# A depthwise convolution whose running sums stand in two PSUM banks, inside a two-layer transformer trunk

## The chip, the cores and the metric

The kernel runs on one core of a Trainium2 chip. The core has a matrix engine (TensorE, "PE" in the profile, with its weight loads as "PEld"), three elementwise engines (VectorE "DVE", ScalarE "ACT", GpSimd "POOL"), a queue engine that starts transfers (SyncE, "SP"), an on-chip memory SBUF and the accumulators PSUM: eight banks, each 128 partitions of 512 fp32 words. Each engine executes its own instructions in program order and waits on semaphores where an operand or a buffer comes from another engine. The metric is the device time of one execution in microseconds (us).

## What is computed

Two layers over 256 tokens of width 1024. Each layer normalises its input and multiplies it by one combined projection matrix. Half of the columns feed an attention of eight heads with three branches (compressed blocks, selected blocks, a sliding window); the other half, 2 × 512 columns, feed a gated causal convolution. Both results go through one output projection, and a channel mixer follows: a dense one in layer 0, one of eight experts in layer 1. The change touches the convolution:

```python
CONV_KERNEL = 31
def conformer_conv(u, conv_w, conv_b, ln_g, ln_b):
    a, g = jnp.split(u, 2, axis=-1)
    h = a * jax.nn.sigmoid(g)
    h = jnp.pad(h, ((0, 0), (CONV_KERNEL - 1, 0), (0, 0)))
    y = lax.conv_general_dilated(h, conv_w[:, None, :], window_strides=(1,), padding='VALID',
                                 dimension_numbers=('NWC', 'WIO', 'NWC'),
                                 feature_group_count=CONV_WIDTH)
    y = y + conv_b
    return jax.nn.silu(layer_norm(y, ln_g, ln_b))
```

Each of the 512 channels is thus a sum of 31 shifted copies of its own row, each times its own weight, and the attention shares with it only the input and the output projection. Of the attention's compressed branch the beginning matters here: the compressed keys and values `kv` are cut into 15 overlapping blocks of 32 tokens and multiplied by a hidden matrix (`compress_blocks`).

## The kernel before, in words

Channels lie on partitions: the 512 channels of the convolution are four chunks `c` of 128 partitions by 256 tokens, in two pairs. TensorE computes the 2 × 256 columns of a pair in 16 steps (`conv_proj`, a step `uA` for pair 0, `uB` for pair 1) into a tile `pu` of two PSUM banks; each step has two chunks of three matmuls (high and low parts, lines 275 to 277). When a pair is complete, `glu` (line 581) writes the gated rows to `hpad` in SBUF.

The 31 taps are divided between two engines. `tap_v` (lines 590 and 593) does the first 17 taps of pair 0 and 16 of pair 1 on VectorE: one instruction multiplies a shifted row of 128 × 256 by a weight per partition and adds the running sum `cv`, in SBUF. `tap_g` does the other taps: ScalarE multiplies (line 602) and GpSimd adds to another sum `cvg` (line 603). `ln_merge` (`lm0`, `lm1`, line 925) adds the two sums of a pair, and a layer norm over channels follows.

Beside this stands the compressed branch. Its projection `pkv` has two banks: the first holds keys and values, ScalarE copies it to `kvc`, and TensorE multiplies this by a permutation (`swap`, line 737) into the second. VectorE copies pieces of both to `blk` (`blk_part`, line 744); 16 × 4 small matmuls `ph` (line 774) follow, and VectorE's `hx` (line 782) reads these. The scores of a step are `S0` to `S11` (tile `pss`, with VectorE's minimum `nm`, line 704), the probabilities `P0` to `P11` (transposes `ptp`, line 844), the values `V0` to `V11` (tile `po`).

The order of all engines in an attention stage is written by hand as a list of tokens, `SEQ`, which is run through once per layer; nothing reorders it. `v` and `g` are one tap each on VectorE and on ScalarE with GpSimd. The PSUM pools have two buffers each: `pa` and `pb` of one bank, `pacc` of two banks (four banks in all). From `pacc` come, in this order, `pkv`, `pu` of pair 0, `pu` of pair 1, the values `po` of the two token blocks and the output projection `pout`. A buffer is given to a new tile when all readers and writers of its last tile are done, and the first instruction that writes the new tile waits for that.

```python
    pacc = ctx.enter_context(tc.tile_pool(name="pacc", bufs=2, space=PSUM))
    def acc_bank(name="acc"):
        return pacc.tile([P, 2, 512], F32, name=name, tag="acc")
    def mm3(dst, ah, al, bh, bl, start, stop, skip=False):
        nc.tensor.matmul(dst, ah, bh, start=start, stop=False, skip_group_check=skip)
        nc.tensor.matmul(dst, ah, bl, start=False, stop=False, skip_group_check=skip)
        nc.tensor.matmul(dst, al, bh, start=False, stop=stop, skip_group_check=skip)
```

In the built program `pkv` stands in banks 4 and 5, `pu` of pair 0 in 6 and 7, and `pu` of pair 1 in 6 and 7 again.

Of the kernel before, what the change touches and what calls it, by code (L numbers as in the profile page):

```python
# [11 lines left out]
F32 = mybir.dt.float32  # L12
# [36 lines left out]
NPT = (0, 0)  # L49
# [6 lines left out]
    P4 S6 P5 v v v g V3 S7 v cs1 g g v cp0 g g S8 g v V4 P6 g g P7 g g join0 S9 cv0 cp1 v V5 v g g V6 v turn0 g g  # L56
    v v v lm0 g V7 oa g P8 g g P9 S10 S11 g V8 v v oa P10 g P11 v v v v V9 v V10 v v lm1 V11 join1 lmean cv1 oa
# [12 lines left out]
def trunk(ctx: ExitStack, tc: tile.TileContext, x, positions, attn_norm_g, ffn_norm_g, w_in, w_out,  # L70
# [397 lines left out]
    for layer in range(DEPTH):  # L468
# [90 lines left out]
        def conv_proj(pair, n):  # L559
            part, k = divmod(n, DK)  # L560
            if n == 0:
                pus[pair] = acc_bank("pu").rearrange("p c (i t) -> p c i t", i=2)
# [42 lines left out]
        pcv = {}  # L605

        def tap_p(pair, j, first, last):

            cs_ = slice(2 * pair, 2 * pair + 2)
            if first:  # L610
                pcv[pair] = bank_a("pcv").rearrange("p (c t) -> p c t", c=2)
            dg = sm.tile([P, 2, P], F32, name="dg", tag="tap", bufs=3)
            nc.gpsimd.tensor_tensor(dg, ident[:, None, :].to_broadcast([P, 2, P]),
                                    cw5[layer][:, cs_, j:j + 1].to_broadcast([P, 2, P]), op=ALU.mult)
            for c in range(2):
                nc.tensor.matmul(pcv[pair][:, c], dg[:, c], hpad[:, 2 * pair + c, j:j + S],
                                 start=(first and c == 0), stop=last, skip_group_check=True)

        vs, gs, ps = [], [], []
# [947 lines left out]
```

## Time and profile before

| | before |
|---|---|
| median of 3 runs | 1595.72 us (1594.69 to 1595.79) |
| the profiled execution | 1595.13 us |
| its span | 1593.3 us |
| busy: TensorE, VectorE, ScalarE, GpSimd | 96%, 84%, 69%, 8% of the span |
| attention stage of layer 0, 40 to 160 us | TensorE 109.36 of 120.00 us busy, VectorE 106.11, ScalarE 75.78, GpSimd 52.73; granted clock 0.86 |
| attention stage of layer 1, 440 to 560 us | TensorE 111.41 of 120.00 us busy, VectorE 106.85, ScalarE 77.04, GpSimd 51.64; granted clock 0.82 |
| dense mixer, 160 to 440 us | TensorE 273.74 of 280.00 us busy |
| experts, 560 to 1593 us | TensorE 1012.81 of 1033.00 us busy |

Times in the trace count from the start of the span; the profiled execution is 1.8 us longer than its span. [...] Busy times overlap between engines. A matmul's recorded length overlaps the next one, so the distance between two starts says more than the length. VectorE's records overlap a little too.

### The profile page before, as it was taken

The page shows a single profiled execution, that of the slowest core. Times are in us where ns is not written, and L with a number is a line of the kernel's source. Part 1 is how long each engine was busy: PE and PEld are TensorE (multiplying, and loading weights), DVE is VectorE, ACT ScalarE, POOL GpSimd, SP SyncE. Part 2 cuts the span into 40 slices and gives each one's busy share as a digit, 9 for nine tenths or more (in the row PEclk, how much of TensorE's full clock was granted, in tenths as well). Part 3 has the DMA queues.
Part 4 walks back from the last instruction along what each step waited for, and adds up shares of the span by engine and source line. Part 5 has one row for each costly group of instructions (what it writes and reads, how often), then busy time and mean ns, then how long its engine had stood idle before and what let it go on. Part 6 is the DMA issues. An engine that isn't in the chain of part 4 may idle for free.

```text
span 1593.3 us, 21310 instructions
## 1 busy us (share of the span) xinstructions
PE 1534.5 (96%) x7833; PEld 1289.9 (81%) x7833; DVE 1337.6 (84%) x1637; ACT 1093.3 (69%) x1430; POOL 122.1 (8%) x152
## 2 busy tenths in 40 slices
PE   6989999999998989999999999999999999999997
PEld 5977799999798768887887887887887887888885
DVE  7898655455689879999999999899999999999996
ACT  5765544444466557787777887787787777778774
POOL 2443000000045300000000000000000000000000
PEclk9978999999997789999999999999999999999999
DMA  9700584555632039999999999999999999999991
GB/s 308 230 28 1 170 315 172 185 186 179 166 122 91 27 120 342 366 367 334 346 369 346 373 370 339 337 361 350 369 369 346 328 362 351 366 369 363 355 371 40
DMA packets 197744, 433.75 MB, mean 272 GB/s; under 512 B 10346, under 2 KB 28978, under 8 KB 197636
## 3 DMA queue, kind: packets, MB, share of 16 engines
q1 hardware_dynamic: 196902, 432.02, 75.8%
q8 instruction: 63, 1.03, 0.3%
q0 software_dynamic: 288, 0.30, 0.1%
q14 instruction: 45, 0.37, 0.1%
q10 hardware_dynamic: 446, 0.03, 0.0%
HBM read 431.27 MB, written 1.05 MB: 271 GB/s over the span
## 4 chain that ended last, share of the span: by engine, by line
PE 80%; DVE 14%; ACT 3%; issue 2%; DMA 1%; POOL 0%; SPq 0%; DVEq 0%; ACTq 0%
PE pg L275 12%; PE pg L277 12%; PE pg L276 12%; PE pd L277 8%; PE pd L276 8%; PE pd L275 7%; DVE cv L593 4%; DVE wl L190 4%; PE pgu L275 3%; PE pgu L277 3%; PE pgu L276 3%; PE pt L288 2%; ACT wh L189 1%; PE pgx L1246 1%; DVE nm L704 1%
## 5 line engine op out<-in xcount | busy, mean ns | idle before, releaser
L190 DVE TENSOR_TENSOR wl<-raw,wh 128x1024 fp32r<-128x1024 f32 x808 | 976.3, 1224 | 176.6 <-ACT wh L189 147.9
L189 ACT CAST wh<-raw 128x1024 fp32r<-128x1024 f32 x808 | 845.4, 1052 | 302.4 <-PE pg L277 102.6
L275 PE MATMUL pg<-wh,xgH 128*128 128x512 f32 x896 | 351.2, 392 | 0.0
L277 PE MATMUL pg<-wh,xgL 128*128 128x512 f32 x896 | 350.6, 391 | 0.0
L276 PE MATMUL pg<-wl,xgH 128*128 128x512 f32 x896 | 349.9, 391 | 0.0
L275 PE MATMUL pd<-wh,fh 128*128 128x512 f32 x560 | 225.8, 403 | 0.1
L276 PE MATMUL pd<-wl,fh 128*128 128x512 f32 x560 | 221.5, 396 | 1.3 <-DVE wl L190 1.3
L277 PE MATMUL pd<-wh,fl 128*128 128x512 f32 x560 | 221.9, 396 | 0.0
L277 PEld LDWEIGHTS pg<-wh,xgL 128*128 128x128 f32 x896 | 168.4, 188 | 35.9 <-DVE xgL L1250 0.2
L276 PEld LDWEIGHTS pg<-wl,xgH 128*128 128x128 f32 x896 | 168.6, 188 | 34.9 <-DVE wl L190 0.3
L275 PEld LDWEIGHTS pg<-wh,xgH 128*128 128x128 f32 x896 | 168.6, 188 | 34.0
L277 PEld LDWEIGHTS pd<-wh,fl 128*128 128x128 f32 x560 | 105.3, 188 | 25.0 <-DVE fl L272 0.2
L276 PEld LDWEIGHTS pd<-wl,fh 128*128 128x128 f32 x560 | 105.4, 188 | 24.6 <-DVE wl L190 2.0
L275 PEld LDWEIGHTS pd<-wh,fh 128*128 128x128 f32 x560 | 105.4, 188 | 22.7 <-ACT fh L271 0.3
L275 PE MATMUL pgu<-hFH,wh 128*128 128x256 f32 x384 | 108.9, 284 | 0.8 <-DVE posT L452 0.8
L277 PE MATMUL pgu<-hFH,wl 128*128 128x256 f32 x384 | 108.7, 283 | 0.0
L276 PE MATMUL pgu<-hFL,wh 128*128 128x256 f32 x384 | 108.7, 283 | 0.0
L603 POOL TENSOR_TENSOR cvg<-cvg,tap 128x256 f32<-128x256 f32 x108 | 93.5, 891 | 80.1 <-ACT tap L602 76.3
L593 DVE SCALAR_TENSOR_TENSOR cv<-hpad,cw,cv 128x256 f32<-128x256 f32 x124 | 75.1, 658 | 0.0
L275 PEld LDWEIGHTS pgu<-hFH,wh 128*128 128x128 f32 x384 | 73.7, 192 | 1.1 <-PE pgk L1080 0.9
L276 PEld LDWEIGHTS pgu<-hFL,wh 128*128 128x128 f32 x384 | 73.7, 192 | 0.2
L277 PEld LDWEIGHTS pgu<-hFH,wl 128*128 128x128 f32 x384 | 73.7, 192 | 0.0
(369 smaller groups left out, 1656.8 us busy)
## 6 DMA issues: line engine op xcount, KB each, us to landing
raw<-in_moe_w_gate_dram SPq DMA_DIRECT2D x112, 1024.0 KB, 5.3
raw<-in_moe_w_up_dram SPq DMA_DIRECT2D x112, 1024.0 KB, 5.4
raw<-in_moe_w_down_dram SPq DMA_DIRECT2D x112, 1024.0 KB, 4.9
raw<-in_w_in_dram SPq DMA_DIRECT2D x18, 1024.0 KB, 9.5
raw<-in_ffn_w_gate_dram SPq DMA_DIRECT2D x14, 1024.0 KB, 7.5
raw<-in_ffn_w_up_dram SPq DMA_DIRECT2D x14, 1024.0 KB, 4.9
raw<-in_ffn_w_down_dram SPq DMA_DIRECT2D x14, 1024.0 KB, 4.9
raw<-in_w_out_dram SPq DMA_DIRECT2D x8, 1024.0 KB, 10.6
```

What stands on the lines that cost most here:

```text
L189: nc.scalar.copy(h, r)
L190: nc.vector.tensor_tensor(lo, r, h.bitcast(F32), op=ALU.subtract)
L275: nc.tensor.matmul(dst, ah, bh, start=start, stop=False, skip_group_check=skip)
L276: nc.tensor.matmul(dst, ah, bl, start=False, stop=False, skip_group_check=skip)
L277: nc.tensor.matmul(dst, al, bh, start=False, stop=stop, skip_group_check=skip)
L288: nc.tensor.transpose(pt[:, k], src[:, k * P:(k + 1) * P], ident)
L593: nc.vector.scalar_tensor_tensor(cv[:, c], src, cw5[layer][:, c, j:j + 1], cv[:, c], op0=ALU.mult, op1=ALU.add)
L603: nc.gpsimd.tensor_tensor(cvg[:, c], cvg[:, c], tap, op=ALU.add)
L704: nc.vector.tensor_reduce(nm, pss, AX.X, ALU.min)
L1246: nc.tensor.matmul(pgx, src[:, b, k * P:(k + 1) * P], ohs[pair][:, b].rearrange("p e s -> p (e s)"), start=(m == 0 and b == 0), stop=(m == ...
```

## The change

The running sums of VectorE, `cv`, are written to a tile `pcv` of two PSUM banks that holds all four chunks. The first call of `tap_v` takes from the pool `pacc` first the tile `pu` of pair 1 and then `pcv`; `conv_proj` then finds the `pu` of pair 1 already there. A new token `leave` ends the use of `pcv`: sums that come after it are written to `cv` in SBUF, and the first one of each chunk reads `pcv`. `lm0` reads pair 0 from `pcv`. In `SEQ`, `leave` and `lm0` with four `v` stand ahead of the token `S8`; `V4` to `V6` and `turn0` have lost the `v` between them, and `lm0` no longer follows `turn0`. A third way of doing taps on TensorE (`tap_p`), whose count `NPT` was zero, is taken out.

```diff
-    P4 S6 P5 v v v g V3 S7 v cs1 g g v cp0 g g S8 g v V4 P6 g g P7 g g join0 S9 cv0 cp1 v V5 v g g V6 v turn0 g g
-    v v v lm0 g V7 oa g P8 ...
+    P4 S6 P5 v v v g V3 S7 v cs1 g g v leave lm0 cp0 v v v v g g S8 g V4 P6 g g P7 g g join0 S9 cv0 cp1 V5 g g V6 turn0 g g
+    v v v g V7 oa g P8 ...
...
-            if n == 0:
+            if n == 0 and pair not in pus:
                 pus[pair] = acc_bank("pu").rearrange("p c (i t) -> p c i t", i=2)
...
+        pcv, sums = {}, {}
+
         def tap_v(c, j):
             src = hpad[:, c, j:j + S]
+            if not pcv:
+                pus[1] = acc_bank("pu").rearrange("p c (i t) -> p c i t", i=2)
+                pcv["t"] = acc_bank("pcv").rearrange("p a (c t) -> p (a c) t", c=2)
+            dst = cv[:, c] if pcv["t"] is None else pcv["t"][:, c]
             if j == 0:
-                nc.vector.tensor_scalar(cv[:, c], src, cw5[layer][:, c, 0:1], cw[layer][:, c, 31:32],
+                nc.vector.tensor_scalar(dst, src, cw5[layer][:, c, 0:1], cw[layer][:, c, 31:32],
                                         op0=ALU.mult, op1=ALU.add)
             else:
-                nc.vector.scalar_tensor_tensor(cv[:, c], src, cw5[layer][:, c, j:j + 1], cv[:, c],
+                nc.vector.scalar_tensor_tensor(dst, src, cw5[layer][:, c, j:j + 1], sums[c],
                                                op0=ALU.mult, op1=ALU.add)
+            sums[c] = dst
+
+        def conv_leave():
+
+            pcv["both"], pcv["t"] = pcv["t"], None
...
         def ln_merge(pair):
             c = slice(2 * pair, 2 * pair + 2)
-            if NPT[pair]:
-                nc.vector.tensor_tensor(cv[:, c], cv[:, c], pcv[pair], op=ALU.add)
-            if NDT[pair] + NPT[pair] < CONV_K:
-                nc.vector.tensor_tensor(cv[:, c], cv[:, c], cvg[:, c], op=ALU.add)
+            assert not vs[pair] and not gs[pair]
+            src = cv[:, c] if pair else pcv["both"][:, c]
+            nc.vector.tensor_tensor(cv[:, c], src, cvg[:, c], op=ALU.add)
```

In the changed program `pkv` stands in banks 4 and 5, `pu` of pair 0 in 6 and 7, `pcv` in 6 and 7 and `pu` of pair 1 in 4 and 5.

TensorE around the start of `pu` of pair 1, with the semaphores each instruction waits for. `pg` is the projection of the gates, `swapm` the permutation of `kvc`. Before:

```order
L275 MATMUL pg<-hTH,wgH_612 24x256
L276 MATMUL pg<-hTL,wgH_612 24x256
L277 MATMUL pg<-hTH,wgL_613 24x256
L737 MATMUL pkv<-kvc,swapm 128x512 [waits Activation_49]
L275 MATMUL pu<-hTH,wh 128x256 [waits DVE_49]
L276 MATMUL pu<-hTL,wh 128x256
L277 MATMUL pu<-hTH,wl 128x256
```

In the changed program:

```order
L274 MATMUL pg<-hTH,wgH_612 24x256
L275 MATMUL pg<-hTL,wgH_612 24x256
L276 MATMUL pg<-hTH,wgL_613 24x256
L731 MATMUL pkv<-kvc,swapm 128x512 [waits Activation_49]
L274 MATMUL pu<-hTH,wh 128x256 [waits DVE_49,PE_49]
L275 MATMUL pu<-hTL,wh 128x256
L276 MATMUL pu<-hTH,wl 128x256
```

The order of the matmuls is the same. The first one into `pu` waited for VectorE's `glu` of pair 0, the last reader of that bank pair; it now waits for the last reader of `pkv`, VectorE's last copy into `blk`.

VectorE from `glu` of pair 0 to that copy. `cw_604` holds the taps' weights, `cw_603` the bias, `posT_616` the position term. Before:

```order
L581 SCALAR_TENSOR_TENSOR hpad<-th,pu 128x256 [waits Activation_49] x2
L590 TENSOR_SCALAR cv<-hpad,cw_604,cw_603 128x256 [waits DVE_49] x2
L593 SCALAR_TENSOR_TENSOR cv<-hpad,cw_604,cv 128x256 [waits DVE_49] x7
L744 COPY blk<-kvc 64x16x15 [waits Activation_49]
L744 COPY blk<-pkv 64x16x15 [waits PE_49]
L744 COPY blk<-pkv 64x16x15
L744 COPY blk<-kvc 64x16x15
L747 COPY blk<-posT_616 128x16
L593 SCALAR_TENSOR_TENSOR cv<-hpad,cw_604,cv 128x256 [waits DVE_49]
L744 COPY blk<-kvc 64x16x15
L744 COPY blk<-pkv 64x16x15 x2
```

In the changed program:

```order
L580 SCALAR_TENSOR_TENSOR hpad<-th,pu 128x256 [waits Activation_49] x2
L596 TENSOR_SCALAR pcv<-hpad,cw_604,cw_603 128x256 [waits DVE_49] x2
L599 SCALAR_TENSOR_TENSOR pcv<-hpad,cw_604,pcv 128x256 [waits DVE_49] x7
L738 COPY blk<-kvc 64x16x15 [waits Activation_49]
L738 COPY blk<-pkv 64x16x15 [waits PE_49]
L738 COPY blk<-pkv 64x16x15
L738 COPY blk<-kvc 64x16x15
L741 COPY blk<-posT_616 128x16
L599 SCALAR_TENSOR_TENSOR pcv<-hpad,cw_604,pcv 128x256 [waits DVE_49]
L738 COPY blk<-kvc 64x16x15
L738 COPY blk<-pkv 64x16x15 x2
```

Nothing moved here; the sums have another tile, and the wait of each on VectorE itself is for the sum right in front of it, where it was for the one two places ahead.

VectorE where `leave` and `lm0` stand, around the probabilities of the compressed branch (`pcmp`, `rsum`, `cfc`) and the minimum of S8. Before:

```order
L884 TENSOR_REDUCE rsum<-pcmp 128x8 [waits Activation_49]
L886 TENSOR_SCALAR cfc<-rsum 128x8 [waits DVE_49]
L887 RECIPROCAL cfc<-cfc 128x8 [waits DVE_49]
L888 TENSOR_TENSOR cfc<-cfc,gate 128x8 [waits DVE_49]
L704 TENSOR_REDUCE nm<-pss 128x2 [waits PE_49]
L593 SCALAR_TENSOR_TENSOR cv<-hpad,cw_604,cv 128x256
```

In the changed program:

```order
L599 SCALAR_TENSOR_TENSOR pcv<-hpad,cw_604,pcv 128x256
L918 TENSOR_TENSOR cv<-pcv,cvg 128x512 [waits DVE_49]
L878 TENSOR_REDUCE rsum<-pcmp 128x8 [waits Activation_49]
L880 TENSOR_SCALAR cfc<-rsum 128x8 [waits DVE_49]
L881 RECIPROCAL cfc<-cfc 128x8 [waits DVE_49]
L882 TENSOR_TENSOR cfc<-cfc,gate 128x8 [waits DVE_49]
L599 SCALAR_TENSOR_TENSOR cv<-hpad,cw_604,pcv 128x256 x2
L599 SCALAR_TENSOR_TENSOR cv<-hpad,cw_604,cv 128x256 [waits DVE_49] x2
L698 TENSOR_REDUCE nm<-pss 128x2 [waits PE_49]
```

The merge and four sums moved ahead of the minimum of S8. On TensorE the first matmul of V4 (`po<-v_sb,prT`), which waited for nothing of VectorE before, now waits for VectorE's second sum after `leave`, the last reader of `pcv`, since `po` of the second token block takes its banks. The other engines' order is the same.

## Rows read from the trace of the kernel before

**Rows 1.** The page's part on the chain that ended last: shares of the span by engine, then by engine, tile and line.

```profile
PE 80%; DVE 14%; ACT 3%; issue 2%; DMA 1%; POOL 0%; SPq 0%; DVEq 0%; ACTq 0%
PE pg L275 12%; PE pg L277 12%; PE pg L276 12%; PE pd L277 8%; PE pd L276 8%; PE pd L275 7%; DVE cv L593 4%; DVE wl L190 4%; PE pgu L275 3%; PE pgu L277 3%; PE pgu L276 3%; PE pt L288 2%; ACT wh L189 1%; PE pgx L1246 1%; DVE nm L704 1%
```

**Rows 2.** Busy time of each engine in the stretch with the second projection and the first half of the taps, in layer 0 and in layer 1: stretch, its length, then busy us (x instructions) of PE, PEld, DVE, ACT, POOL, the granted clock, the share of the DMA engines, GB/s.

```profile
62.00:88.50 26.50, 26.16 (x184) 25.10 (x182) 26.39 (x40) 16.15 (x34) 18.64 (x20) 0.83 0.37 125
463.30:491.40 28.10, 27.70 (x185) 26.91 (x184) 27.95 (x45) 19.02 (x43) 18.64 (x20) 0.78 0.30 102
```

**Rows 3.** The timeline of TensorE and VectorE where TensorE first stands idle, four rows of layer 0 and three of layer 1: start, duration of the group, engine, line, operation, tiles, shape, count, and in brackets the idle time ahead and what ended it.

```profile
88.84 1.42 PE L844 MATMUL ptp<-ident,sc 128*128 128x128 f32 x4 [0.32 <-DVE gate L757]
90.05 3.46 PE L774 MATMUL ph<-blk,raw 128*128 128x31 f32 x16
95.24 0.22 DVE L782 COPY hx<-ph 128x62 f32<-128x62 f32 x1
95.47 1.11 PE L844 MATMUL ptp<-ident,sc 128*128 128x128 f32 x4 [1.96 <-ACT prT L846]
...
492.24 2.11 PE L774 MATMUL ph<-blk,raw 128*128 128x31 f32 x16
496.88 0.21 DVE L782 COPY hx<-ph 128x62 f32<-128x62 f32 x1
497.11 1.12 PE L844 MATMUL ptp<-ident,sc 128*128 128x128 f32 x4 [2.77 <-ACT prT L846]
```

**Rows 4.** The timeline of TensorE at the start of `pu` of pair 1, with the same columns; the last row is that of layer 1.

```profile
61.97 0.68 PE L275 MATMUL pu<-hTH,wh 128*128 128x256 f32 x1
62.49 0.28 PE L276 MATMUL pu<-hTL,wh 128*128 128x256 f32 x1
...
463.28 0.68 PE L275 MATMUL pu<-hTH,wh 128*128 128x256 f32 x1
```

**Rows 5.** The timeline of VectorE from the first sum to the last copy out of `pkv`, with the same columns; the last row is that copy in layer 1.

```profile
61.26 0.73 DVE L590 TENSOR_SCALAR cv<-hpad,cw,cw 128x256 f32<-128x256 f32 x2
61.90 4.30 DVE L593 SCALAR_TENSOR_TENSOR cv<-hpad,cw,cv 128x256 f32<-128x256 f32 x7
...
69.12 1.03 DVE L593 SCALAR_TENSOR_TENSOR cv<-hpad,cw,cv 128x256 f32<-128x256 f32 x1
70.08 0.36 DVE L744 COPY blk<-kvc 64x240 f32<-64x240 f32 x1
70.45 0.82 DVE L744 COPY blk<-pkv 64x240 f32<-64x240 f32 x2
...
471.77 0.82 DVE L744 COPY blk<-pkv 64x240 f32<-64x240 f32 x2
```

**Rows 6.** The timelines of GpSimd's additions and of two groups of sums on VectorE, one beside them and one where GpSimd has none; the same columns.

```profile
63.12 6.75 POOL L603 TENSOR_TENSOR cvg<-cvg,tap 128x256 f32<-128x256 f32 x8 [15.02 <-ACT tap L602]
70.63 12.02 POOL L603 TENSOR_TENSOR cvg<-cvg,tap 128x256 f32<-128x256 f32 x12 [0.76 <-ACT tap L602]
```
```profile
73.35 3.58 DVE L593 SCALAR_TENSOR_TENSOR cv<-hpad,cw,cv 128x256 f32<-128x256 f32 x4
...
84.39 2.05 DVE L593 SCALAR_TENSOR_TENSOR cv<-hpad,cw,cv 128x256 f32<-128x256 f32 x5
```

**Rows 7.** The timeline of VectorE at two operations of the compressed scores, of which the second reads what the first writes.

```profile
115.29 0.29 DVE L870 TENSOR_TENSOR scmp<-psc,scmp 128x128 f32<-128x128 f32 x1
115.61 0.29 DVE L872 TENSOR_REDUCE mncmp<-scmp 128x8 f32<-128x128 f32 x1
```

**Rows 8.** All the running sums, and the scaling of the layer norm, whose operand `prs` is in PSUM: line, engine, operation, tiles, count, duration of one in ns (minimum, median, maximum), first and last start.

```profile
L593 DVE SCALAR_TENSOR_TENSOR cv<-hpad,cw,cv x124: 463/479/1046, 61.9 to 540.3; 128x256 f32<-128x256 f32 x124
L955 DVE SCALAR_TENSOR_TENSOR cv<-cv,cw,prs x8: 473/475/482, 147.3 to 551.3; 128x256 f32<-128x256 f32 x8
```

**Rows 9.** TensorE's clock: two pairs of neighbouring matmuls of `pu` in the timeline, then the busy times and the granted clock (the third number from the end) of two stretches of layer 0 and two of layer 1.

```profile
74.35 0.28 PE L276 MATMUL pu<-hTL,wh 128*128 128x256 f32 x1
74.46 0.28 PE L277 MATMUL pu<-hTH,wl 128*128 128x256 f32 x1
...
86.39 0.41 PE L275 MATMUL pu<-hTH,wh 128*128 128x256 f32 x1
86.61 0.41 PE L276 MATMUL pu<-hTL,wh 128*128 128x256 f32 x1
```
```profile
80.00:84.00 4.00, 4.00 (x19) 3.79 (x19) 4.00 (x6) 0.51 (x1) 2.65 (x4) 0.50 0.03 6
88.80:93.50 4.70, 4.66 (x20) 4.14 (x20) 4.70 (x11) 3.89 (x18) 2.46 (x3) 0.50 0.01 3
488.70:491.40 2.70, 2.70 (x14) 2.70 (x15) 2.67 (x9) 1.85 (x10) 0.00 (x0) 0.50 1.04 400
491.40:494.50 3.10, 2.95 (x21) 2.83 (x20) 3.10 (x5) 2.62 (x12) 2.46 (x3) 0.79 0.46 175
```

**Rows 10.** The timeline of layer 0 behind `hx`: three groups of VectorE's sums, and TensorE's output projection with the idle time ahead of it.

```profile
98.04 0.92 DVE L590 TENSOR_SCALAR cv<-hpad,cw,cw 128x256 f32<-128x256 f32 x1
109.78 1.35 DVE L593 SCALAR_TENSOR_TENSOR cv<-hpad,cw,cv 128x256 f32<-128x256 f32 x2
111.65 2.31 DVE L593 SCALAR_TENSOR_TENSOR cv<-hpad,cw,cv 128x256 f32<-128x256 f32 x3
...
128.34 0.50 PE L277 MATMUL pout<-wh,mixL 128*128 128x512 f32 x1 [1.43 <-DVE mixL L272]
```

More of the change, by code (lines that the diff above doesn't have):

```diff
@@ L48 @@
 NDT = (17, 16)
-NPT = (0, 0)
 SEQ = """
@@ L55 @@
     P0 ph3 v g P1 gelu v g S2 heads v g g g v g P2 S3 S4 cnorm V0 g v v V1 v keys v g S5 v g P3 cs0 v g g v V2 g
-    P4 S6 P5 v v v g V3 S7 v cs1 g g v cp0 g g S8 g v V4 P6 g g P7 g g join0 S9 cv0 cp1 v V5 v g g V6 v turn0 g g
-    v v v lm0 g V7 oa g P8 g g P9 S10 S11 g V8 v v oa P10 g P11 v v v v V9 v V10 v v lm1 V11 join1 lmean cv1 oa
+    P4 S6 P5 v v v g V3 S7 v cs1 g g v leave lm0 cp0 v v v v g g S8 g V4 P6 g g P7 g g join0 S9 cv0 cp1 V5 g g V6 turn0 g g
+    v v v g V7 oa g P8 g g P9 S10 S11 g V8 v v oa P10 g P11 v v v v V9 v V10 v v lm1 V11 join1 lmean cv1 oa
     lvar turn1 lscale oa oa lout oa oa oa
@@ L603, in tap_g @@
                 nc.gpsimd.tensor_tensor(cvg[:, c], cvg[:, c], tap, op=ALU.add)
[L605 to L619, printed above, removed]
+        vs, gs = [], []
         for pair in range(2):
             nd = NDT[pair]
-            ng = nd + NPT[pair]
             vs.append([lambda c=c, j=j: tap_v(c, j) for j in range(nd) for c in (2 * pair, 2 * pair + 1)])
-            ps.append([lambda pair=pair, j=j, nd=nd, ng=ng: tap_p(pair, j, j == nd, j == ng - 1)
-                       for j in range(nd, ng)])
-            gs.append([lambda c=c, j=j, ng=ng: tap_g(c, j, j == ng) for j in range(ng, CONV_K)
+            gs.append([lambda c=c, j=j, nd=nd: tap_g(c, j, j == nd) for j in range(nd, CONV_K)
                        for c in (2 * pair, 2 * pair + 1)])
@@ L1000, in trunk @@
                  "oc": [lambda k=k, b=b: out_conv(k, b) for b in range(NB) for k in range(4)],
-                 "p": [lambda: some(ps, 1)] * (2 * CONV_K),
                  "v": [lambda: some(vs, 1)] * (4 * CONV_K), "g": [lambda: some(gs, 1)] * (4 * CONV_K),
@@ L1023, in trunk @@
         events += [("gelu", cmp_gelu), ("heads", cmp_heads), ("cnorm", cmp_norm), ("keys", cmp_keys)]
-        events += [("lm0", lambda: ln_merge(0)), ("lm1", lambda: ln_merge(1)), ("lmean", ln_mean), ("lvar", ln_var), ("lscale", ln_scale), ("lout", ln_out)]
+        events += [("leave", conv_leave), ("lm0", lambda: ln_merge(0)), ("lm1", lambda: ln_merge(1)), ("lmean", ln_mean), ("lvar", ln_var), ("lscale", ln_scale), ("lout", ln_out)]
         for b in range(NB):
```

## The prediction

> **What bounds the kernel now.** I read the chain of waits first [rows 1]. It gives TensorE 80% of the span and VectorE 14%, and names the running sums of the convolution (`cv`, line 593) with 4%, as if they were worth shortening. An average over stages can't say that, so I read the table of busy time for the stage in which the sums stand. From 62.00 to 88.50 TensorE is busy 26.16 of 26.50 us and VectorE 26.39; in layer 1, from 463.30 to 491.40, 27.70 and 27.95 of 28.10 [rows 2]. Both are full. Which one decides is seen in the order of time. TensorE's first idle of more than a trace is 0.32 us at 88.84; the next that counts is 1.96 us ahead of 95.47, and in layer 1 2.77 us ahead of 497.11 [rows 3]. Up to there VectorE is late, but TensorE has other work in its order and loses nothing. What VectorE saves before 88.8 therefore buys at most the little that TensorE waits for it: 0.32 us, and the time by which VectorE's `hx` is behind the matmuls `ph` that feed it, 95.24 − (90.05 + 3.46) = 1.73 us; in layer 1 496.88 − (492.24 + 2.11) = 2.53 us [rows 3]. I call these the slack: 2.05 us in layer 0, 2.5 in layer 1.
>
> **The change part by part.** *1. The buffers.* The pool of accumulators has two buffers of two banks. Before, the bank pair of `pkv` stays with the compressed keys while the second projection `pu` takes the pair that the first has left, so TensorE starts it at 61.97 (layer 1: 463.28) [rows 4]. The changed order gives that pair to `pcv`, and the second `pu` gets the pair of `pkv`. Its first matmul now waits for VectorE's last read of `pkv`. In the order this copy stands behind two sums that begin a chunk, eight that go on, and the other copies into `blk`; in the trace it ends at 70.45 + 0.82 = 71.27, in layer 1 at 471.77 + 0.82 = 472.59 [rows 5]. TensorE works in order, so everything behind that matmul (the rest of `pu`, the gates, the transposes, S0, `ph`) stands as well.
>
> How long: VectorE's own work ahead of the copy changes too. Seven sums take 4.30 us and one takes 0.96 until the copy behind it starts (69.12 to 70.08) [rows 5]. They contend with GpSimd's additions `cvg`: without these a sum comes each 0.40 us (five from 84.39 in 2.05, the last being 0.47 long), beside them each 0.88 (four from 73.35 in 3.58) [rows 6]. In the changed order each sum waits for the one right in front of it, because four chunks share one tile, where before it waited for the one two places ahead. A dependent operation follows after its full length and 0.03 us (115.29, 0.29 long, to 115.61) [rows 7], so I take 0.48 + 0.03 = 0.51 for each sum into PSUM, with no contention. Seven then take 3.57 (−0.7), the single one 0.40, as a copy from another tile follows it (−0.56), the two that begin a chunk 0.24 more than the 0.64 between 61.26 and 61.90 [rows 5]. Together −1.0: the copy ends at 70.2. The stall is 70.2 − 61.97 = 8.3, less 0.4, since the matmul that leads now costs 0.52 to the next (61.97 to 62.49) [rows 4] and only some 0.12 once it starts warm: **7.9 us** in layer 0; in layer 1 472.59 − 1.0 − 463.28 = 8.3, and also 7.9.
>
> No row shows a VectorE sum into PSUM. The nearest is line 955, which reads one operand from PSUM: 473, 475 and 482 ns at minimum, median and maximum, against a median of 479 for the sums in SBUF, which go up to 1046 [rows 8]. So the length is taken as 0.48 and the contention as gone. Bounds: no serialization (0.40 apart) makes the stall 1.0 shorter, the contended pace of 0.88 makes it 3.8 longer (nine sums by 0.37, and the start).
>
> [...]
>
> *2. What the stall is worth.* The slack takes its part: 7.9 − 2.05 = 5.85 in layer 0, 7.9 − 2.5 = 5.4 in layer 1. VectorE, which was late, uses the stall to catch up, so `hx` then follows `ph` at once.
>
> *3. TensorE's clock.* Nowhere else in the two attention stages does TensorE stand for nearly 8 us. [...] I expect the lower level after such a pause. How soon the upper returns with dense `pu` work is seen in layer 1: from 488.70 to 491.40 the granted clock is 0.50 and from 491.40 to 494.50 0.79 on average, which is 2.7 + 3.1 × 0.42 = 4.0 us at the lower level [rows 9]. Four microseconds hold 18 matmuls at 0.22, and 18 × (0.215 − 0.12) is **1.75 us** per layer. Bounds: 0, and the lower level through all 96 matmuls of the second `pu`, 9.1 us.
>
> *4. Sums behind the stall.* From 95 us on VectorE sets the pace. The start of a chunk at 98.04 takes 0.92 where it takes 0.41 alone; two sums at 109.78 take 1.35 and three at 111.65 2.31, against 0.88 and 1.28 at 0.40 apart [rows 10]: −0.5 − 0.5 − 1.0 = −2.0 if PSUM ends contention. Five dependent sums in this stretch at +0.11 give 0.55 back. **−1.4 us** per layer; layer 1 taken as the same.
>
> *5. The merge and four sums, moved.* `lm0` and four sums go from behind V5, V6 and the first transposes to ahead of S8. Their number is the same, and V4 and the minimum of S8 come later by the merge, 0.6, and four sums, 1.6, which the 1.4 and the later gap repay; cost 0. Bounds for 4 and 5 together: +0.7 per layer less gain (S8 waits and nothing comes back), and −2.8 in all if also TensorE's 1.43 us ahead of 128.34 [rows 10] goes. The first matmul of V4 now waits for VectorE's second sum, which is over long before: 0. The first sum of each chunk after `leave` reads PSUM once: 0 by line 955 [rows 8].
>
> The sum: layer 0 5.85 + 1.75 − 1.4 = 6.2, layer 1 5.4 + 1.75 − 1.4 = 5.75, **+11.9 us**. The profiled execution took 1595.13 (a span of 1593.3 and 1.8 around it); 1595.1 + 11.9 = 1607.0. That execution is 0.6 under the median of the runs, so against the median I say **1607.6**.
>
> **Rivals.** *A: the contention decides, and TensorE's wait is absorbed.* For: the chain of waits names the sums, and a contended sum costs twice as much as one alone [rows 1, 6]. Then the slack and the later gain are won: 2.05 + 1.4 + 2.5 + 1.4 = 7.4, 1588.3 against the median. Against: the slack at the first matmul of the second `pu` is minus 9.3 us (61.97 against 71.27) [rows 4, 5], and nothing stands ahead of it in TensorE's order. It decides only if VectorE reaches the copy 8 us sooner.
> [...]
> *B: no change.* If TensorE, shifted by the stall, kept the upper level through the 13.5 us from 80 to 93.5 that it now spends at 0.50 [rows 9], it would win 13.5 × (1 − 0.12 / 0.215) = 5.9 per layer: about 1595.8. For: the stall puts more dense `pu` work among the narrow matmuls. Against: the fall at 80 comes with `ph` and its 31 columns, which are the same.
> *C: much slower.* Sums into PSUM go at the contended pace (+3.8 per layer) or the lower clock lasts through the second `pu` (+7.4): 1615 to 1625. For: no row shows VectorE writing PSUM while TensorE is half clocked.
> That `pcv` takes another place, so that no wait arises, the order of the built program excludes.
>
> **How the numbers follow.** Forecast 79%, A 5%, B 6%, C 10%. Low end: no serialization −2.0, no clock loss −3.5, late gain −2.8, in all −8.3 from 1607.6: 1599.3, so 1600. High end: the contended pace for both layers +7.6 and the late loss +1.4 with no more clock loss give 1616.6, so 1617; what is left out is A, B and half of C. One measurement of this kernel tells no change from one of about 0.2%, 3.2 us. Faster than that: A, 0.05. Within: B and a little, 0.07. Slower: 0.88.
>
> **What would show it.** In the trace after: an idle of TensorE of about 8 us ahead of the first matmul of the second `pu` in both layers, ended by VectorE's copy of `pkv`; the granted clock near 0.5 just behind it; sums of 0.48 us at 0.51 apart, none near 0.9, beside GpSimd's additions; `hx` within a fraction of a microsecond after `ph`; `nm` of S8 no later relative to `ph` than before. The prediction is wrong if that idle is under 5 us, if the sums into PSUM take 0.6 or more, or if TensorE regains over 5 us in the stretch up to `hx`.

## The result: the changed kernel is 0.5% slower

| | before | changed |
|---|---|---|
| median | 1595.32 us (4 runs, 1594.69 to 1595.79) | 1603.11 us (4 runs, 1601.89 to 1607.02) |
| ratio | | 1.0052, interval 1.0037 to 1.0067 |
| profiled execution | 1595.13 us, span 1593.3 | 1602.85 us, span 1601.1 |

The forecast was 1607.6 us, with a range of 1600 to 1617. The direction, the range and the first wait came out. The medians differ by 7.8 us; by the ratio the change costs 8.3 us, which is the figure used below. As the experiments show, the size came out in part by luck: several terms were wrong and partly cancelled, and about 3 of the 8.3 us lie at the end of the program, where the forecast had nothing.

### The profile after

The idle time of TensorE by what ended it, 40 to 160 us of the changed kernel (engine, tile and line that waited, what it waited for, us in total, times, longest), the first three lines:

```profile
PE pu L274 <- DVE blk L738: 8.0, 1, 8.0
PE po L853 <- DVE cv L599: 3.7, 1, 3.7
PE ptp L838 <- DVE kcsq L805: 1.1, 1, 1.1
...
```

The first line is the forecast stall. The second, ahead of V4, I had priced at nothing. Next comes the timeline of the stall, first that of TensorE (answering [rows 4], with layer 1's row last), then that of VectorE ([rows 5]):

```profile
62.25 1.13 PE L731 MATMUL pkv<-kvc,swapm 128*128 128x512 f32 x2 [0.82 <-ACT kvc L728]
71.41 0.55 PE L274 MATMUL pu<-hTH,wh 128*128 128x256 f32 x1 [8.03 <-DVE blk L738]
...
476.87 0.55 PE L274 MATMUL pu<-hTH,wh 128*128 128x256 f32 x1 [8.04 <-DVE blk L738]
```
```profile
62.21 1.13 DVE L596 TENSOR_SCALAR pcv<-hpad,cw,cw 128x256 f32<-128x256 f32 x2
63.38 3.64 DVE L599 SCALAR_TENSOR_TENSOR pcv<-hpad,cw,pcv 128x256 f32<-128x256 f32 x7
66.93 0.73 DVE L738 COPY blk<-kvc 64x240 f32<-64x240 f32 x1
...
69.69 0.48 DVE L599 SCALAR_TENSOR_TENSOR pcv<-hpad,cw,pcv 128x256 f32<-128x256 f32 x1
70.08 0.34 DVE L738 COPY blk<-kvc 64x240 f32<-64x240 f32 x1
70.44 0.82 DVE L738 COPY blk<-pkv 64x240 f32<-64x240 f32 x2
```

TensorE stands until VectorE's last copy out of `pkv` ends at 70.44 + 0.82 = 71.26. This profile is 0.8 us behind that of before already at the first `pu` (46.02 after 45.20), where nothing was changed. Seven sums take 3.64 us; with 0.49 for the last one they start (3.64 − 0.49) / 6 = 0.525 apart, close to the forecast 0.51.

All the sums by tile, answering [rows 8], and the first operation of each chunk:

```profile
L599 DVE SCALAR_TENSOR_TENSOR pcv<-hpad,cw,pcv x92: 470/490/491, 63.4 to 523.9; 128x256 f32<-128x256 f32 x92
L596 DVE TENSOR_SCALAR pcv<-hpad,cw,cw x8: 542/545/548, 62.2 to 507.5; 128x256 f32<-128x256 f32 x8
L599 DVE SCALAR_TENSOR_TENSOR cv<-hpad,cw,cv x28: 469/474/960, 124.4 to 546.0; 128x256 f32<-128x256 f32 x28
```

The 92 sums into PSUM take at most 491 ns, though GpSimd's additions run beside many of them. The 28 that are still in SBUF go up to 960 ns, as in [rows 8]. Where the slack was to be, answering [rows 3]:

```profile
100.29 2.31 PE L768 MATMUL ph<-blk,raw 128*128 128x31 f32 x16
102.44 0.64 PE L838 MATMUL ptp<-ident,sc 128*128 128x128 f32 x4
...
102.64 0.22 DVE L776 COPY hx<-ph 128x62 f32<-128x62 f32 x1 [0.79 <-PE ph L768]
```

`hx` starts 0.04 us after `ph` ends, and VectorE has been waiting for it; the idle of 1.96 us ahead of `ptp` is gone.

How far each instruction is behind the same one of before shows where the time goes, since the order of the matmuls is the same. In layer 0 this lag is 0.83 us at the first `pu`, 11.78 behind the stall (65.67, now 77.45), 7.40 at `hx` (95.24, now 102.64) and 4.8 at the last `pout` (168.03, now 172.82). In layer 1 it is 4.99 at the first `pu` (447.41, now 452.40), 14.70 behind the stall (465.45, now 480.15), 8.47 at `hx` (496.88, now 505.35) and 4.6 at the last `pout` (570.30, now 574.91). So in these two profiles layer 0 loses 4.0 us, and layer 1 wins back all that the stall cost.

In the timeline around V4, VectorE's row group with the second sum after `leave` ends what TensorE waits for:

```profile
121.81 0.69 DVE L918 TENSOR_TENSOR cv<-pcv,cvg 128x512 f32<-128x512 f32 x1
...
123.62 0.86 DVE L599 SCALAR_TENSOR_TENSOR cv<-hpad,cw,pcv 128x256 f32<-128x256 f32 x2
...
124.53 1.75 PE L853 MATMUL po<-v_sb,prT 128*128 128x64 f32 x7 [3.67 <-DVE cv L599]
```

TensorE's clock: the stall, the dense work behind it, and two later stretches, then both attention stages as a whole, of the changed kernel; columns as in [rows 2], the granted clock third from the end. That clock is a share of TensorE's full speed; in both traces a stretch without a change of level reads 1.00 or 0.50, and other values are means over both:

```profile
67.50:71.40 3.90, 0.00 (x0) 0.02 (x1) 3.79 (x10) 0.48 (x1) 2.25 (x3) 0.50 0.00 0
71.40:77.30 5.90, 5.89 (x27) 5.73 (x28) 3.44 (x7) 0.18 (x1) 0.00 (x0) 0.50 0.53 171
77.40:91.40 14.00, 14.00 (x121) 13.92 (x119) 10.05 (x16) 11.96 (x28) 10.31 (x12) 0.98 0.24 78
91.50:101.30 9.80, 9.80 (x47) 9.59 (x47) 6.50 (x14) 3.95 (x17) 2.10 (x3) 0.50 0.01 2
...
57.00:172.00 115.00, 98.62 (x582) 85.96 (x581) 92.41 (x191) 70.89 (x184) 45.12 (x59) 0.85 0.13 46
456.00:575.00 119.00, 102.98 (x642) 90.66 (x640) 95.70 (x199) 74.16 (x190) 45.12 (x59) 0.89 0.24 80
```

and the kernel before, its long stretch at the lower level and the same two stages:

```profile
79.80:103.60 23.80, 20.49 (x87) 17.80 (x87) 21.88 (x48) 11.45 (x41) 9.94 (x15) 0.50 0.14 45
...
57.00:172.00 115.00, 103.25 (x590) 88.01 (x589) 102.56 (x197) 74.77 (x190) 49.66 (x59) 0.85 0.13 48
456.00:575.00 119.00, 109.59 (x641) 96.03 (x639) 104.35 (x201) 76.14 (x194) 48.57 (x59) 0.81 0.21 72
```

The clock falls during the stall (0.50 from 67.1 on, 3.7 us after TensorE came to stand) and comes back 5.9 us after it: the forecast loss. In layer 1 it comes back 3.3 us after it (476.87 to 480.15). Later the clock gives time back: the stretch at the lower level that lasted 23.8 us lasts 9.8, and in layer 1 the mean rises from 0.81 to 0.89. The time that a stage spends at 0.50 is 2 × (1 − clock) × length: before, the two stages held 34.5 + 45.2 = 79.7 us of it, now 34.5 + 26.2 = 60.7. The clock has two digits here, so each of these figures is good to about 1 us. In layer 0 the later gain just makes up for the stall; the whole difference is in layer 1.

**The account by the traces.** Summing the idle times ahead of TensorE's matmuls from the first `pu` to the last `pout`, layer 0 goes from 10.8 to 16.4 us and layer 1 from 8.6 to 16.0: +13.0 us. The 19.0 us less at the lower level are, at 0.12 us a matmul instead of 0.215 [rows 9], worth 19.0 × 0.44 = 8.4. That leaves +4.6; the last matmul of the kernel starts 4.55 us later (1585.76, now 1590.31). That the two agree so closely is in part chance: 0.8 of the 4.55 was there at the first `pu`, and part of the lower level falls into the idle times, where it costs nothing (13.5 us in the changed kernel, 6.8 before). But the span is 7.8 us longer. The rest, 3.2 us, lies behind the last matmul. These are the last pieces of the chain (start, us, what) and the spans, before and changed:

```profile
1586.27 0.68 DVE xt L1428
...
span 1593.3 us, 21310 instructions
```
```profile
1590.82 0.68 DVE xt L1420
...
span 1601.1 us, 21306 instructions
```

From the end of that piece to the end of the span it is 6.4 us before and 9.6 now. There are four instructions fewer, all of them semaphore waits in TensorE's queue (two of the four also go in e_seq below, which changes the order alone). In the closing sequence TensorE's queue now stands from 1596.07 to 1598.93 between two semaphore instructions; before, these follow one another every 0.11 us. The page's part on the queues has one more instruction transfer, 64 (1.05 MB) for 63 (1.03 MB), and one such transfer of 16 KB runs inside this stand, from 1596.29 to 1597.41.

### The profile page after: what moved, and what is told of

It reads as the page before. It is cut to its first block, busy times and chain, and to the rows that moved or that the text cites. A ratio compares the mean times of both kernels' runs of the same rounds, so it can differ in the third digit from the quotient of the medians.

```text
span 1601.1 us, 21306 instructions
## 1 busy us (share of the span) xinstructions
PE 1527.6 (95%) x7833; PEld 1284.6 (80%) x7833; DVE 1324.6 (83%) x1637; ACT 1092.7 (68%) x1430; POOL 114.1 (7%) x152
## 3 DMA queue, kind: packets, MB, share of 16 engines
q8 instruction: 64, 1.05, 0.3%
HBM read 431.27 MB, written 1.05 MB: 270 GB/s over the span
## 4 chain that ended last, share of the span: by engine, by line
PE 85%; DVE 10%; ACT 2%; issue 1%; DMA 1%; POOL 0%; SPq 0%; DVEq 0%; ACTq 0%
PE pg L274 12%; PE pg L276 12%; PE pg L275 12%; PE pd L276 7%; PE pd L275 7%; PE pd L274 7%; PE pgu L274 3%; PE pgu L276 3%; PE pgu L275 3%; DVE wl L189 3%; PE pt L287 2%; ACT wh L188 1%; DVE pcv L599 1%; PE ph L768 1%; DVE cv L599 1%
## 5 line engine op out<-in xcount | busy, mean ns | idle before, releaser
L614 POOL TENSOR_TENSOR cvg<-cvg,tap 128x256 f32<-128x256 f32 x108 | 85.8, 819 | 94.3 <-ACT tap L613 94.0
L274 PE MATMUL pu<-hTH,wh 128*128 128x256 f32 x128 | 40.2, 314 | 16.1 <-DVE blk L738 16.1
## 6 DMA issues: line engine op xcount, KB each, us to landing
raw<-in_w_out_dram SPq DMA_DIRECT2D x8, 1024.0 KB, 10.4
```

The source lines that it names most:

```text
L614: nc.gpsimd.tensor_tensor(cvg[:, c], cvg[:, c], tap, op=ALU.add)
```

## The experiments

Times are medians in us. "Before" was run again on the chip of each batch, and the ratio is to that. A difference between two of these ratios is uncertain by about 3 us.

| run | median | before there | ratio (interval) |
|---|---|---|---|
| the change | 1603.11 | 1595.32 | 1.0052 (1.0037 to 1.0067) |
| e_pad | 1599.96 | 1595.69 | 1.0034 (1.0020 to 1.0047) |
| e_early | 1592.47 | 1595.69 | 0.9976 (0.9967 to 0.9985) |
| e_stall | 1606.23 | 1595.69 | 1.0065 (1.0052 to 1.0078) |
| e_seq | 1604.63 | 1595.69 | 1.0052 (1.0039 to 1.0065) |
| e_swap | 1587.68 | 1597.27 | 0.9943 (0.9927 to 0.9959) |
| e_leave2 | 1599.38 | 1597.27 | 1.0017 (1.0005 to 1.0028) |
| e_banks | 1601.38 | 1597.27 | 1.0029 (1.0016 to 1.0042) |
| e_best | 1585.76 | 1597.27 | 0.9930 (0.9916 to 0.9943) |
| e_ctl | 1597.19 | 1595.83 | 1.0012 (1.0002 to 1.0022) |
| e_best2 | 1585.97 | 1595.83 | 0.9935 (0.9921 to 0.9949) |

**The end of the program (e_pad).** The changed kernel with one more one-column matmul per layer. The profile counts it as two weight loads and two matmuls, so TensorE's queue has eight instructions more than the change, not the four that I expected:

```diff
+            for _ in range(1):
+                nc.tensor.matmul(pv[:, 4:5], ln["sq"][:, 0, 0:P], ones[:, 0:1], start=True, stop=True)
```

> The changed kernel with one more one-column matmul per layer ahead of the variance's square root, whose result nothing reads: four more instructions in TensorE's queue, as many as the change took out (waits). In the trace after, TensorE's queue stands 2.9 us in the closing sequence, between two semaphore instructions, which the trace before does not show there; the last work ends 4.5 us later than before, the span 7.8 us. Theory T (the stall on pkv makes up the stages, and the rest is where the queue's instructions lie at the end): the gap in the closing sequence goes, the time falls by about 3 us, to 1600 (1599 to 1601). Rival (the end has nothing to do with the count of instructions): no change, 1603.

Measured 1599.96, 3.2 under the change (by the ratio 2.9; the two intervals overlap). Its span ends 6.6 us after the chain's last piece:

```profile
1589.04 0.63 DVE xt L1422
...
span 1596.3 us, 21314 instructions
```

The theory holds by the profile: in the profiled execution 3 us of the result are no matter of the convolution but of the closing sequence, and are gone with eight instructions more in TensorE's queue. All later runs carry such matmuls (their lines are left out of the edits below), or have TensorE's waits of before, and all end 7.7 to 7.9 us after the start of the last matmul; the kernel before takes 7.6, and the change alone 10.8. The other runs are therefore to be read against e_pad rather than against the change.

**Taking the stall away, first way (e_early).** The changed kernel with the copies into `blk` ahead of the sums:

```diff
-    setup uA uA gt gt gt kx0 uA uA uA kx1 gt qx0 uA uA uA kt10 uA uA uA uA uA v kvo gt kt00 ...
-    v g v swap blk1 g v blk0 uB ...
+    setup uA uA gt gt gt kx0 uA uA uA kx1 kvo gt qx0 uA swap uA uA kt10 blk1 uA uA blk0 uA uA uA v gt kt00 ...
+    v g v g v uB ...
```

> The changed kernel with the copy kvc, the swap and the copies into blk moved ahead of the first sums, so that the second pu finds pkv's banks free; two more one-column matmuls per layer whose result nothing reads keep TensorE's queue as long as before. Theory T (the stall on pkv is what costs): TensorE's idle of 8 us goes, and with it 4 to 6 us of the stages' loss per layer or more; with the end as before: 1590 to 1595, not slower than the kernel before. Rival R (the stall is absorbed, and the sums into PSUM, each waiting for the one ahead, and the wait of V4 cost the time): 1599 to 1601, as with the closing gap alone removed.

Measured 1592.47, which is 7.5 under e_pad and faster than before. An idle of 3.7 us is left, since the copies now stand ahead of the gating, whose second row TensorE waits for:

```profile
66.96 0.58 PE L274 MATMUL pu<-hTH,wh 128*128 128x256 f32 x1 [3.71 <-DVE hpad L580]
```

**Second way (e_swap).** The changed kernel, order untouched; the swap has a bank of its own, so ScalarE's copy alone holds `pkv`:

```diff
-            nc.tensor.matmul(kvg["p"][:, 1], later["swapm"], kvg["kvc"], start=True, stop=True)
+            kvg["sw"] = bank_b("psw")
+            nc.tensor.matmul(kvg["sw"], later["swapm"], kvg["kvc"].rearrange("p i t -> p (i t)"), start=True, stop=True)
...
-                    src = kvg["kvc"] if kv == half else kvg["p"][:, 1]
+                    src = kvg["kvc"] if kv == half else kvg["sw"].rearrange("p (i t) -> p i t", i=2)
```

> The changed kernel with the swap written to a tile of its own from the one-bank pool, so that pkv's pair comes free with ScalarE's copy kvc and no copy into blk holds it; order of tokens unchanged; two more one-column matmuls per layer whose result nothing reads. The run with earlier copies into blk still showed 3.7 us of idle ahead of the second pu, since blk stood ahead of the gating there. Theory T (the 8 us idle costs): no idle over 1 us there, time 3 us or more under that run's 1592.5 or about the same if a later transpose waits for the new bank instead: 1586 to 1592. Rival R (the idle is absorbed, what was won came from elsewhere): 1592 to 1600.

Measured 1587.68, 0.57% under before. The second `pu` no longer waits; part of the idle comes back further on, as allowed for, and the wait of V4 stays:

```profile
71.58 0.63 PE L552 MATMUL pqT<-ident,qst 128*128 128x128 f32 x4 [2.27 <-DVE blk L739]
...
115.83 1.97 PE L854 MATMUL po<-v_sb,prT 128*128 128x64 f32 x8 [3.67 <-DVE cv L599]
```

Between e_swap and e_pad lies the stall with its clock, less the 2.27 us per layer that came back: 1.0034 − 0.9943 = 0.0091, or 14.5 us. The forecast of 14.75 (5.85 + 5.4 + 2 × 1.75) is not the figure to set beside it. The forecast had taken the slack off, and both of these kernels have the faster sums, which win the slack without a stall. In the forecast's terms the stall alone is 2 × (7.9 + 1.75) = 19.3, and 14.8 without the 4.5 that came back.

**The stall alone (e_stall).** The kernel before, sums in SBUF; a spare tile pushes the second `pu` into the banks of `pkv`:

```diff
...
+            if pair == 1 and n == 1:
+                nc.vector.tensor_copy(qss[0][:, 0:1], spare["t"][:, 0, 0:1])
...
+            if not spare:
+                pus[1] = acc_bank("pu").rearrange("p c (i t) -> p c i t", i=2)
+                spare["t"] = acc_bank("spare")
+                nc.vector.memset(spare["t"][:, 0, 0:1], 0.0)
```

> The kernel before, sums in SBUF and order of tokens unchanged; a spare tile takes the bank pair of the first pu at the first sum and is read once after the second pu has begun, so that the second pu must take pkv's banks. Theory T: an idle of TensorE of 9.0 us ahead of the second pu (VectorE's last copy stands at 71.3), a lower clock behind it, and 4 to 7 us per layer after what is absorbed: 1602 to 1609. Rival R: 1595 to 1597, since TensorE waits for VectorE later anyway.

Measured 1606.23, which is +10.4 us, and an idle of 8.78:

```profile
72.34 0.55 PE L275 MATMUL pu<-hTH,wh 128*128 128x256 f32 x1 [8.78 <-DVE blk L750]
```

The stall costs without any change to the sums. The rival that it is absorbed is out.

**The order alone (e_seq).** The kernel before with `lm0` and four `v` where the change has them:

```diff
-    ... cs1 g g v cp0 g g S8 g v V4 ... cp1 v V5 v g g V6 v turn0 g g
-    v v v lm0 g V7 ...
+    ... cs1 g g v lm0 cp0 v v v v g g S8 g V4 ... cp1 V5 g g V6 turn0 g g
+    v v v g V7 ...
```

> The kernel before with the tokens lm0 and four v moved as in the change, sums in SBUF, and one more one-column matmul per layer whose result nothing reads. Theory T: within 1.5 us of before, 1594 to 1597, as the same work stands elsewhere and V4 waits for nothing of VectorE. Rival R: the moved work delays the minimum of S8 by 2.2 us per layer: 1599 to 1600.

Measured 1604.63, which is +8.3 us: both theories were wrong. Where before has 1.63 us ahead of `poc`, TensorE now stands

```profile
125.51 1.22 PE L894 MATMUL poc<-vblk,pcT 128*128 128x512 f32 x1 [4.55 <-ACT prT L846]
...
531.80 2.07 PE L894 MATMUL poc<-vblk,pcT 128*128 128x512 f32 x2 [4.45 <-ACT prT L846]
```

since the minimum of S8, and with it the probabilities, come later. That wait is about 3 us longer in each layer. In layer 0 other waits are shorter, and the sum of TensorE's idle times stays at 10.2 us (before 10.8); there the loss goes with the clock, whose lower level holds 51 us of the stage instead of 34.5. In layer 1 the idle times grow from 8.6 to 15.6 us, and the lower level holds 40.5 us instead of 45.2. Why the order alone moves the clock is not shown.

**The order in the changed kernel (e_leave2).** `leave` and `lm0` earlier, the four `v` at their old places:

```diff
-    P4 S6 P5 v v v g V3 S7 v cs1 g g v leave lm0 cp0 v v v v g g S8 g V4 ... cp1 V5 g g V6 turn0 g g
+    P4 S6 P5 leave lm0 v v v g V3 S7 v cs1 g g v cp0 g g S8 g v V4 ... cp1 v V5 v g g V6 v turn0 g g
```

> The changed kernel with leave and lm0 earlier, behind P5, and the four sums back at their old places behind V5, V6 and the first transposes; one more one-column matmul per layer whose result nothing reads. In the trace after, TensorE stands 3.67 us ahead of V4, until VectorE's second sum after leave; in the run of the moved tokens with sums in SBUF it stood 4.5 us ahead of poc, where before has 1.3 to 1.6, and lost 3 to 5 us per layer behind V4. Theory V (the merge and the sums ahead of V4 and of S8's minimum cost 3 us per layer): the idle ahead of V4 goes, 1592 to 1596, against 1600 with the closing gap alone removed. Rival (VectorE sets that stretch whatever its order, and the same idle appears further on): 1598 to 1601.

Measured 1599.38, beside a before of 1597.27. Theory V expected 1592 to 1596 and is wrong. Against e_pad the ratio is lower by 0.0017, 2.7 us, but the intervals overlap. The wait of V4 is gone, and others are back in its place, much as the rival has it; of the idle from 40 to 160 us the longest are:

```profile
PE pu L274 <- DVE blk L738: 8.0, 1, 8.0
PE poc L888 <- ACT prT L840: 1.6, 1, 1.6
PE ptp L838 <- ACT pcT L877: 1.1, 1, 1.1
```

**Sums that need not wait for one another (e_banks).** The chunks of a pair in different banks:

```diff
-                pcv["t"] = acc_bank("pcv").rearrange("p a (c t) -> p (a c) t", c=2)
-            dst = cv[:, c] if pcv["t"] is None else pcv["t"][:, c]
+                pcv["t"] = acc_bank("pcv").rearrange("p a (h t) -> p a h t", h=2)
+            dst = cv[:, c] if pcv["t"] is None else pcv["t"][:, c % 2, c // 2]
...
```

> The changed kernel with the chunks of a pair in different banks of pcv, so that a sum no longer waits for the one right in front of it; one more one-column matmul per layer whose result nothing reads. Theory T: sums 0.40 apart instead of 0.525, the last copy out of pkv and with it the second pu 0.9 us earlier (idle 7.1 instead of 8.0), and about 1 us per layer more later on: 1596 to 1599. Rival (the sums are not what sets the pace): idle 7.1, but the time stays at 1599.5 to 1601.

Measured 1601.38. The edit does not do what it was meant to: five sums still take 2.59 us, which is 0.525 apart, so each still starts only when the one in front has ended, whichever bank it is in, and the idle is 8.04 us, as without the edit. So it tells nothing of the waits among the sums. It is a second run of e_pad, and agrees with it (1.0029 and 1.0034).

**All together (e_best), and the place of the sums by itself (e_ctl).** e_best is the edits of e_swap, e_leave2 and e_banks in one. e_ctl is the kernel before with the swap's edit of e_swap and the early `lm0`, so with sums in SBUF:

```diff
-    P4 S6 P5 v v v g V3 ...
-    v v v lm0 g V7 ...
+    P4 S6 P5 lm0 v v v g V3 ...
+    v v v g V7 ...
```

> All three edits together: swap in a tile of its own, leave and lm0 behind P5 with the four sums at their old places, chunks of a pair in different banks; two more one-column matmuls per layer whose result nothing reads. Theory T with V: no idle of TensorE over 1.5 us in the stage; the sums no longer contend, so faster than before: 1582 to 1589. Rival R: 1590 to 1596.

> The kernel before, sums in SBUF, with two edits of the run with all three: the swap in a tile of its own from the one-bank pool, and lm0 behind P5; one more one-column matmul per layer whose result nothing reads. No stall on pkv and no wait of V4 in either; what is left between the two is where the sums stand. Theory P (sums in PSUM, which don't contend with GpSimd, are worth 8 us or more once nothing waits for their banks): 1594 to 1600, within 0.3% of before. Rival Q (the gain of 11 us came from the order and the swap's tile): 1585 to 1589.

e_best takes 0.9930 of before, e_ctl 1.0012. In neither does the second `pu` wait for `pkv`, or V4 for VectorE; what differs is where the sums stand, and that is worth 0.0082, or 13 us. That is theory P. e_best came in the expected range, but three idles over 1.5 us, which it was not to have, are left in each layer: 2.8 (layer 1: 2.9) ahead of transposes `ptp`, 2.3 ahead of `qt10`'s and 1.6 ahead of `poc`.

**One wait less (e_best2).** As e_best, with the chunks where the change has them and `qt10` two `uB` later:

```diff
-    ... uB uB g gt v uB qt10 g uB v uB v g ...
+    ... uB uB g gt v uB g uB v qt10 uB v g ...
```

> As the run with all three edits, with the chunks' places in pcv as in the change (the other places left the waits as they were), and qt10 two uB steps later: TensorE stood 2.28 us ahead of qt10's transposes there, since the swap's tile holds their bank until blk is copied. Theory: that idle falls under 1 us, 1 to 2 us per layer less, 1582 to 1585. Rival (VectorE or the clock takes it back): 1585 to 1587.

Measured 1585.97, a ratio of 0.9935: the idle ahead of `qt10` falls from 2.3 to 1.6 us, and the time stays, as the rival said. The next two views show how e_ctl (first) and e_best2 (second) differ. Each has the sums (all 124 in SBUF, or the 82 that go into PSUM), GpSimd's additions, and both stages (columns as in [rows 2]):

```profile
L593 DVE SCALAR_TENSOR_TENSOR cv<-hpad,cw,cv 128x256 f32<-128x256 f32 x124 | 73.5, 645 | 0.0
...
L603 POOL TENSOR_TENSOR cvg<-cvg,tap 128x256 f32<-128x256 f32 x108 | 91.7, 873 | 86.8 <-ACT tap L602 85.9
...
57.00:172.00 115.00, 104.77 (x602) 91.67 (x600) 101.81 (x198) 74.35 (x189) 48.98 (x59) 0.84 0.13 46
456.00:575.00 119.00, 104.15 (x621) 91.11 (x620) 100.07 (x197) 73.50 (x189) 47.49 (x59) 0.86 0.22 76
```
```profile
L599 DVE SCALAR_TENSOR_TENSOR pcv<-hpad,cw,pcv 128x256 f32<-128x256 f32 x82 | 39.9, 487 | 2.0
...
L614 POOL TENSOR_TENSOR cvg<-cvg,tap 128x256 f32<-128x256 f32 x108 | 85.0, 814 | 80.2 <-ACT tap L613 79.9
...
57.00:172.00 115.00, 105.01 (x612) 91.27 (x611) 99.07 (x202) 75.73 (x191) 45.85 (x60) 0.88 0.13 47
456.00:575.00 119.00, 103.68 (x633) 90.36 (x632) 101.40 (x215) 78.64 (x198) 48.04 (x61) 0.86 0.21 72
```

A sum takes 487 ns on average in PSUM and 645 in SBUF, and each of GpSimd's additions is 59 ns shorter on average. TensorE's idle times, summed as above, fall from 25.1 to 17.7 us, and the time at the lower level from 70.1 to 60.9, which at 0.44 is 4.0: together 11.4 of the 12.5 us by which the last matmul comes earlier. In the one profile of each run, the two stages hold 51 to 61 us at the lower level in all eight kernels with sums in PSUM and 70 to 91 in the four with sums in SBUF.

## Why the prediction was right, and where it was not

The account by runs goes in steps, from the kernel before to the change: the swap's bank and the early `lm0`, with sums in SBUF, +1.9 us (e_ctl); sums in PSUM −12.3 (e_best2 against e_ctl); the moved order with V4's wait +1.3 (e_swap against e_best2; e_pad against e_leave2 gives +2.7, and neither is clear of noise); the stall with its clock +14.5 (e_pad against e_swap); the closing sequence +2.9 (the change against e_pad). They add to +8.3. In the forecast's own terms the sums were to give −7.4 (rival A's sum), the stall +19.3, and the other steps nothing, in all +11.9. Since e_swap keeps 4.5 us of idle of its own, the split between the sums and the stall is uncertain by about that much.

- *Step 1, the buffers: right.* The wait is where it was put, ended by the copy named, in both layers. I said 7.9 us and it is 8.03 and 8.04.
- *Step 1, the pace of the sums: right.* They start 0.525 apart for 0.51, without contention. The first operation of a chunk takes 545 ns into PSUM, 0.1 us more than I took, and the copies ahead of `pkv`'s are still drawn out (0.73 at 66.93, against 0.34 at 70.08). The sums into PSUM are 11 ns longer than those in SBUF (medians of 490, and 479 before), and the four that read PSUM and write SBUF are not (469).
- *Step 2, the slack: right where I looked, too small as a bound.* `hx` follows `ph` at once, and the idle that was VectorE's there is gone. But I took the slack, 2.05 and 2.5 us, as the most that VectorE's saving could buy up to there. By the lag, TensorE regains 11.78 − 7.40 = 4.4 us from the stall to `hx` in layer 0 and 14.70 − 8.47 = 6.2 in layer 1. Over 5 us there was one of the three signs by which the prediction would be wrong: in layer 1 it came. The other two (an idle under 5 us, sums of 0.6 or more) did not.
- *Step 3, the clock: half.* Behind the stall the loss is as forecast: the lag grows from 9.44 us at the first matmul of the second `pu` (61.97 and 71.41) to 11.78 (65.67 and 77.45) in layer 0, and from 13.59 (463.28 and 476.87) to 14.70 (465.45 and 480.15) in layer 1. That is 2.3 and 1.1 us for 1.75 each (the forecast's 18 × 0.095 gives 1.71, with 0.12 us from one `pu` matmul to the next at the upper level and 0.215 at the lower [rows 9]). No row of before had shown that a pause brings the lower level; that was expected, and in the changed kernel it came 3.7 us into the stall, in layer 1 4.4. But I looked no further. Over both stages the lower level lost 19 us, a gain of 8.4. It goes with the place of the sums rather than with the stall, since in the profiles at hand all kernels with sums in PSUM show it. Rival B, to which I gave 6%, had the mechanism, at another place: the fall while `ph` runs is still there (at 91.0, for 79.7 before) and the return comes sooner, after some 10 us for 24.
- *Step 4, sums behind the stall: the wrong size, with step 2.* I forecast −1.4 us per layer, from three contended groups that I could point at behind 95 us, and let the low end of the range have 2.8 more in all. With the slack of step 2 that makes 7.4 for the place of the sums, where the runs give 12 to 13. The step that failed stands in the first part: that what VectorE saves buys at most the time that TensorE now waits for it. It leaves out that the time spent at the lower clock also shrinks, in the same kernels. Rival A stated this 7.4, and was wrong in denying the stall. That the contention ends in PSUM was right, though it was an estimate: GpSimd adds nothing beside line 955, so no row of before showed it. In the changed kernel a sum into PSUM takes 491 ns at most, where one in SBUF took up to 1046 before, and GpSimd's additions are shorter too (873 ns on average in e_ctl, 814 in e_best2).
- *Step 5, the moved merge and sums: wrong.* I said that V4's wait "is over long before". By VectorE's order the sum stands behind the merge and four small operations of the softmax, and TensorE waits 3.67 us for it. The time is repaid, as the idles of 1.22, 1.63 and 1.43 us behind it go. With sums in SBUF the same order costs 8.3 us.
- *The end: missed.* The change has four waits fewer in TensorE's queue, and 2.9 us went in its closing sequence. The trace has one instruction transfer more (64 for 63), and one such transfer inside the stand; but the kernel before has one among the same semaphores (from 1591.55) and no stand. That TensorE stood for this transfer is not shown by any run, only that eight instructions more remove the stand.

So the range held with some luck. By the steps above, sums and stall together came to +2.2 us where I had +11.9, and what I had at nothing (e_ctl's step, the order, the end) came to +6.1. Without the closing sequence, as in e_pad, the change costs 5.4 us, about half of the +11.9 forecast. Nor was layer 1 the same as layer 0: in the profiles it loses nothing, where I had +5.75. What stays open: what the waits among the sums cost, since the edit meant to remove them left the pace as it was; and which part of the gain in PSUM is TensorE's clock, since the two go together in every run.

## What to carry to other kernels

A tile that moves into a pool shifts every later tile of that pool; look for the first instruction whose buffer's last reader now stands behind other work on its engine. Here that one wait turned a gain of 0.6% (e_swap) into a loss of 0.3% (e_pad), and a bank of its own for one small matmul took it back. Price a change without its new waits too, with the clock over the whole stage: a saving on an engine that "has slack" may still shorten the time that TensorE spends at its lower level (here 51 to 61 us in the two stages, for 70 to 91). And when a difference of a few microseconds is left over, look behind the last useful instruction.

## What the runs showed of the hardware that I had not expected

- Three microseconds at the end hang on a few instructions in TensorE's queue: 10.8 us from the last matmul to the end with 21306 instructions in the profile (the change), 7.6 with 21310 (before) and 7.8 with 21314 (e_pad).
- In the changed kernel a sum whose running value is in PSUM takes the same 490 ns beside GpSimd as alone (470 to 491 over all 92); before, with all 124 in SBUF, the median was 479 and the longest took 1046.
- e_pad and the change are the same program up to the layer norm, and yet in layer 0 the last matmul of the second `pu` is 2.1 us earlier in e_pad's profile (97.09 for 99.23), though its stall ends 0.65 us later (72.06 for 71.41). The upper level is back 3.3 us after the stall instead of 5.9, and lost again at 92.5 instead of 91.0. A profile of one execution carries that much chance per layer here.
